# A transformer block on one core: from the fourth unit on, the feed-forward reads the finished second norm in 256 columns instead of the unscaled x in 258

## The chip, the cores and the metric

The kernel runs on one core of a Trainium2 chip, as one program with one launch. The metric is the time of one execution on the device in microseconds. A core has a matrix engine (TensorE; PE in the profile, PEld for its weight loads), a vector engine (VectorE; DVE), a scalar engine (ScalarE; ACT), GpSimd (POOL) and the queue of the sync engine that issues the loads (SP).

## The reference, cut to what matters

One block over 256 tokens with 1024 features, in float32: a modulated mixing part (attention and a gated unit), and then the feed-forward that the change touches:

```
x = x + gate1 * (merged @ w_out)
h = rmsnorm(x, g_ffn) * (1 + scale2) + shift2
x = x + gate2 * (square(relu(h @ w_ff1)) @ w_ff2)      # w_ff1: 1024 x 4096
return rmsnorm(x, g_final)
```

`rmsnorm` divides each token by the root of the mean square of its features, so `h` can only be finished when all features of `x` are known; `scale2` and `shift2` are one number per feature.

## The kernel before, in words

All data lie transposed: features on the 128 partitions in 8 tiles (`KT`), the 256 tokens along the row. To keep float32 accuracy each operand of a product is split in a rounded high part and a low remainder, and each product is three matmuls, high by high, high by low, low by high (`mm3`, line 72). The weights come as 1 MB pieces of 128 x 2048 in a fixed order of "slots": a load from the SP queue into one of five `raw` buffers, a cast to the high part on ScalarE (`high`, line 240, four buffers), and a subtraction on VectorE for the low part (`low`, line 249, three buffers). `prepare(slot + 2)` issues the low part of the slot after next and the high part of the one two further.

The feed-forward has 16 units of 256 hidden features. A unit has a first product (`ff1`, line 619: 8 feature tiles x 2 halves x 3 = 48 matmuls), an activation (`relu2` and `relu2_low`, lines 630 and 644) and a second product (`ff2`, line 651, 48 matmuls) that adds into four PSUM banks which stay for all units. On TensorE the order is: first products of units 1, 2, 3, then in turn second product of unit 1, first of unit 4, second of unit 2, first of unit 5, and so on. In the loop of line 683 iteration n holds the second product of unit n+1 and the first of unit n+4.

The first products don't wait for the norm. They read `zh`, `zl`: `x` times the norm's gain and (1 + scale2), not divided by the root, with 2 columns more per row (258): column 256 holds `shift2`, so that the matmul also gives the product of the shift, and column 257 is zero. Each half of the unit has its own bank. `relu2` mends the rest behind the product: it copies the shift's column out of the bank (`bw`), multiplies the bank by the tokens' factor `rb2` on VectorE, adds `bw` in a Relu on ScalarE, squares on ScalarE into `r2`, and casts that to `fh`; `relu2_low` makes the remainder `fl` on VectorE. `rb2` is there from the middle of the second unit's first product on (`spread2`).

`wide` (line 404) is the same product over rows of 256 columns, with both halves in one bank; the earlier stages use it, the output projection with `mh`, `ml`, which lie in the places `b1` and `b2`.

In this part the instructions are not pinned to the order of the program: a planner orders each engine's queue ahead of time, by the order of the program among what it takes to be ready. An engine then works off its queue in that order.

Of the kernel before, what the change touches and what calls it, by code (L numbers as in the profile page):

```python
# [9 lines left out]
F32 = mybir.dt.float32  # L10
F32R = mybir.dt.float32r
BF16 = mybir.dt.bfloat16
AF = mybir.ActivationFunctionType
ALU = mybir.AluOpType
AX = mybir.AxisListType

P = 128
S = 256
D = 1024
KT = D // P  # L20
# [27 lines left out]
def block_kernel(ctx, tc, x, xT, cols, wsguT, bsgu, w_a1, w_1, w_a, w_m, w_f, out):  # L48
    nc = tc.nc
    PE, DVE, ACT = (InOrder(tc, e) for e in (nc.tensor, nc.vector, nc.scalar))  # L50
    const = ctx.enter_context(tc.tile_pool(name="const", bufs=1))
    act = ctx.enter_context(tc.tile_pool(name="act", bufs=1))
    wk = ctx.enter_context(tc.tile_pool(name="wk", bufs=2))
# [6 lines left out]
    def bank():  # L60
        return ps.tile([P, 512], F32, name="bank", tag="bank")
# [8 lines left out]
    def mm3(out, wh, wl, ah, al, first, last, **kw):  # L70
        PE.matmul(out=out, lhsT=wh, rhs=ah, start=first, stop=False, **kw)
        PE.matmul(out=out, lhsT=wh, rhs=al, start=False, stop=False, **kw)
        PE.matmul(out=out, lhsT=wl, rhs=ah, start=False, stop=last, **kw)
# [11 lines left out]
    x_sb = act.tile([P, KT, S], F32, name="x_sb")  # L85
# [11 lines left out]
    def spin(n):  # L97
# [13 lines left out]
        out=maskf, in_=maskf, pattern=[[0, 2], [-1, P]], compare_op=ALU.is_ge,  # L111
# [60 lines left out]
    acol = const.tile([P, 2, KT], F32, name="acol")  # L172
    bcol = const.tile([P, 2, KT], F32, name="bcol")
    gcol = const.tile([P, 2, KT], F32, name="gcol")
    pre = const.tile([P, 2, KT], F32, name="pre")
    for n, (sc, g) in enumerate(((SCALE1, G_MIX), (SCALE2, G_FFN))):
        DVE.scalar_tensor_tensor(
            out=pre[:, n], in0=cols_sb[:, sc:sc + KT], scalar=1.0, in1=cols_sb[:, g:g + KT],
            op0=ALU.add, op1=ALU.mult)
# [60 lines left out]
    def high(n):  # L240
        if n < NM + 2 * NU:
            raw = fetch("w", n)
            hi = his.tile([P, 2048], F32R, name="whi", tag="whi")
            m = 2048 // pieces(n)
            for i in range(pieces(n)):
                ACT.copy(out=hi[:, m * i:m * i + m], in_=raw[:, m * i:m * i + m])
            his_of[n] = raw, hi

    def low(n):
        if n < NM + 2 * NU:  # L250
            raw, hi = his_of.pop(n)
            lo = los.tile([P, 2048], F32R, name="wlo", tag="wlo")
            m = 2048 // pieces(n)
            for i in range(pieces(n)):
                w = slice(m * i, m * i + m)
                DVE.tensor_tensor(out=lo[:, w], in0=raw[:, w], in1=hi[:, w].bitcast(F32), op=ALU.subtract)
            parts[n] = hi, lo

    def prepare(n):
        low(n)  # L260
        high(n + 2)

    def ada_dots(m, half):
        i = (0, 4, 1, 5, 2, 6, 3, 7, 8, 9, 10, 11, 12, 13, 14, 15)[m]
        if half == 0:
            raw_of["d", m] = fetch("a", m)
        raw = raw_of["d", m]
        column(dot(raw, half), (SCALE2, GATE1, SHIFT2, GATE2)[i // 4], 2 * (i % 4) + half)
# [11 lines left out]
    for kt in range(KT):  # L280
        f, l = kt == 0, kt == KT - 1
# [8 lines left out]
        hf = wk.tile([P, S], F32, name="hf", tag="hf", bufs=2)  # L290
        wp = [slice(2048 // np_ * i, 2048 // np_ * (i + 1)) for i in range(np_)]
        xk = xps[0][:, 0:S] if f else xn[:, kt]
        a, b = acol[:, 0, kt:kt + 1], bcol[:, 0, kt:kt + 1]
# [110 lines left out]
    def wide(n, ah, al, nk, base=0):  # L404

        wh, wl = parts[n]
        o = bank()
        for ko in range(nk):
            for i in range(2):
                w = slice(base + 256 * ko + P * i, base + 256 * ko + P * i + P)  # L410
                mm3(o[:, S * i:S * i + S], wh[:, w], wl[:, w], ah[:, ko], al[:, ko],
                    ko == 0 and i == 0, ko == nk - 1, skip_group_check=i == 1)
        return o
# [87 lines left out]
    sc, ex, tp, po, zo = {}, {}, {}, {}, {}  # L501
    A0, S0, TD, OD = 1, 5, 2, 3
    for n in range(10):
# [9 lines left out]
        if n == 2:  # L513
            nc.sync.dma_start(out=wsg, in_=wsguT)
            for i in range(2):
                nc.sync.dma_start(
                    out=bsg[64 * i:64 * i + 64],
                    in_=bass.AP(tensor=bsgu.tensor, offset=128 * i, ap=[[0, 64], [256, NP], [1, P]]))
            nc.gpsimd.affine_select(
                out=wsg, in_=wsg, pattern=[[0, 8], [1, P]], compare_op=ALU.is_ge,  # L520
# [9 lines left out]
        o = wide(n, hh, hl, KT)  # L530
# [18 lines left out]
        if n < 2:  # L549
            dst, func, scale = u_sb[:, 2 * n:2 * n + 2], AF.Gelu_apprx_tanh, 1.0  # L550
        else:
            dst, func, scale = (ga_sb, gb_sb)[m // 4][:, 2 * (m % 4):2 * (m % 4) + 2, 0:S], AF.Tanh, 0.5
# [5 lines left out]
    for j in range(4):  # L558
        n = 10 + j
        prepare(n + 2)  # L560
        t = []
        if n in AT:
            ada_dots(AT.index(n), 0)
        for k, (ah, al, g) in enumerate(((oh, ol, ga_sb), (yh, yl, gb_sb))):
            o = wide(n, ah, al, 4, 1024 * k)
            y = wk.tile([P, 2, S], F32, name="yg", tag=f"t512{'ab'[k]}")
            DVE.scalar_tensor_tensor(out=y, in0=g[:, 2 * j:2 * j + 2, 0:S], scalar=1.0,
                                     in1=o.rearrange("p (i t) -> p i t", i=2), op0=ALU.add, op1=ALU.mult)
# [15 lines left out]
    for j in range(4):  # L584
        n = 14 + j
# [4 lines left out]
        o = wide(n, mh, ml, KT)  # L590
# [5 lines left out]
        fts = (2 * j, 2 * j + 1)  # L596
        for ft in fts:
            i = ft % 2
            DVE.scalar_tensor_tensor(
                out=x_sb[:, ft], in0=o[:, S * i:S * i + S], scalar=gcol[:, 0, ft:ft + 1], in1=x_sb[:, ft],  # L600
                op0=ALU.mult, op1=ALU.add)
# [3 lines left out]
        for ft in fts:  # L605
            DVE.scalar_tensor_tensor(
                out=zl[:, ft, 0:S], in0=x_sb[:, ft], scalar=acol[:, 1, ft:ft + 1],
                in1=zh[:, ft, 0:S].bitcast(F32), op0=ALU.mult, op1=ALU.subtract)
# [7 lines left out]
    rb2 = const.tile([P, S], F32, name="rb2", tag="m1")  # L616
    slot = NM

    def ff1(n, half=None):
        wh, wl = parts[n]  # L620
        o = [bank(), bank()]
        for ko in range(KT):
            for i in range(2):
                w = slice(256 * ko + P * i, 256 * ko + P * i + P)
                mm3(o[i][:, 0:ZW], wh[:, w], wl[:, w], zh[:, ko], zl[:, ko], ko == 0, ko == KT - 1)
            if ko == 3 and half:
                half()
        return o

    def relu2(o):  # L630
        r = wk.tile([P, 2, S], F32, name="r", tag="t512a")
        bw = small.tile([P, 2], F32, name="bw", tag="bw")
        r2 = wk.tile([P, 2, S], F32, name="r2", tag="t512b")
        fh = wk.tile([P, 6 * P], F32R, name="fh", tag="pr", bufs=3)[:, 0:512].rearrange("p (i t) -> p i t", i=2)
        for i in range(2):
            DVE.tensor_copy(out=bw[:, i:i + 1], in_=o[i][:, S:S + 1])
            DVE.tensor_tensor(out=r[:, i], in0=o[i][:, 0:S], in1=rb2, op=ALU.mult)
        for i in range(2):
            ACT.activation(out=r[:, i], in_=r[:, i], func=AF.Relu, bias=bw[:, i:i + 1])
        ACT.activation(out=r2, in_=r, func=AF.Square)  # L640
        ACT.copy(out=fh, in_=r2)
        return r2, fh

    def relu2_low(r2, fh):
        fl = wk.tile([P, 6 * P], F32R, name="fl", tag="pt")[:, 0:512].rearrange("p (i t) -> p i t", i=2)
        DVE.tensor_tensor(out=fl, in0=r2, in1=fh.bitcast(F32), op=ALU.subtract)
        return fh, fl

    acc = []

    def ff2(n, fts, wp, a, first, last):
        wh, wl = wp
        fh, fl = a
        if not acc:
            acc.extend(bank() for _ in range(4))
        for ft in fts:
            o = acc[ft // 2][:, S * (ft % 2):S * (ft % 2) + S]
            for i in range(2):
                w = slice(1024 * i + P * ft, 1024 * i + P * ft + P)
                mm3(o, wh[:, w], wl[:, w], fh[:, i], fl[:, i], first and i == 0 and ft % 2 == 0,  # L660
                    last and i == 1, skip_group_check=ft % 2 == 1)

    f = {}
    a = {}
# [13 lines left out]
    a[0] = relu2(f.pop(0))  # L678
    slot += 1
    prepare(slot + 2)  # L680
    a[1] = relu2(f.pop(1))
    a[0] = relu2_low(*a[0])
    f[2] = ff1(slot)
    slot += 1
    for n in range(NU - 2):
        prepare(slot + 2)
        a[n + 1] = relu2_low(*a[n + 1])
        if n in (1, 3, 5, 7):
            ada_dots(12 + n // 2, 0)
        ff2(n, range(KT), parts[slot], a.pop(n), n == 0, False)  # L690
        a[n + 2] = relu2(f.pop(n + 2))
        slot += 1
        if n + 3 < NU:
            prepare(slot + 2)
            if n in (1, 3, 5, 7):
                ada_dots(12 + n // 2, 1)
            f[n + 3] = ff1(slot)
            slot += 1
    a[NU - 1] = relu2_low(*a[NU - 1])

# [6 lines left out]
    for j in range(4):  # L707
        fts = (2 * j, 2 * j + 1)
# [3 lines left out]
        for i, ft in enumerate(fts):  # L712
            DVE.scalar_tensor_tensor(out=x_sb[:, ft], in0=acc[j][:, S * i:S * i + S], scalar=gcol[:, 1, ft:ft + 1],
                                     in1=x_sb[:, ft], op0=ALU.mult, op1=ALU.add)
# [84 lines left out]
```

## Time and profile before

| | |
|---|---|
| time, median of 3 runs | 362.6 us (362.24 to 362.86) |
| time of the profiled execution | 363.53 us |
| span of the profiled execution, first to last instruction | 360.8 us |
| TensorE busy | 350.1 us, 97% of the span, 2898 matmuls |
| VectorE busy | 259.3 us, 72% |
| ScalarE busy | 216.7 us, 60% |
| GpSimd busy | 9.2 us, 3% |
| TensorE's mean granted clock | 0.996 of full speed (2.4 GHz) |

Busy times are sums of the union of an engine's instructions over the span; the shares are averages over stages with different limits. The duration of one matmul in the rows (0.28 us) holds its way through the array, and the next starts before it ends: what a stream of matmuls costs is read from the distance of their starts.

### The profile page before, as it was taken

To read this page: it belongs to the slowest core of one execution; us is meant where nothing else is said; L and a number is where in the kernel's file an instruction comes from. 1 tells how busy PE (TensorE), PEld (TensorE's weight loads), DVE (VectorE), ACT (ScalarE), POOL (GpSimd) and SP (SyncE) were. 2 spreads that over 40 slices of the span, in tenths; PEclk is the share of its full clock that TensorE was granted. 3 is DMA by queue.
4 is the path that set the end of the run, shared out by engine and by line. 5 is a ranking of instruction groups with operands and counts; after the bars stand their busy time and mean duration, and the time that the engine had idled before them with its cause. 6 is when DMAs were issued, how large, how long until landed. Compare 5 with 4: busy or idle time off the path is not lost.

```text
span 360.8 us, 6952 instructions
## 1 busy us (share of the span) xinstructions
PE 350.1 (97%) x2898; PEld 338.8 (94%) x2898; DVE 259.3 (72%) x403; ACT 216.7 (60%) x308; POOL 9.2 (3%) x16
## 2 busy tenths in 40 slices
PE   6999999999999999999999999999999999999993
PEld 5688989999999999999999999999999999999993
DVE  4898986689799988999858665576665654645443
ACT  5867679899954563555576554466544664446242
POOL 3000000003000000000000000000000000000001
PEclk9999999999999999999999999999999999999998
DMA  7999999699898896478554665746758464500003
GB/s 241 417 411 411 410 400 420 221 369 369 336 385 320 308 382 233 182 261 328 225 184 167 234 250 217 288 179 243 252 207 295 173 234 155 196 2 0 2 0 116
DMA packets 16270, 90.39 MB, mean 251 GB/s; under 512 B 1904, under 2 KB 2416, under 8 KB 7152
## 3 DMA queue, kind: packets, MB, share of 16 engines
q1 hardware_dynamic: 16240, 89.97, 66.4%
q8 instruction: 22, 0.36, 0.4%
q14 instruction: 8, 0.07, 0.1%
HBM read 88.91 MB, written 1.05 MB: 249 GB/s over the span
## 4 chain that ended last, share of the span: by engine, by line
PE 87%; DMA 6%; DVE 2%; issue 1%; SPq 1%; ACT 1%; POOLq 0%; POOL 0%; DVEq 0%
PE bank L44 87%; DMA raw<-in_w 3%; DMA raw<-in_w_a 3%; SPq L67 1%; DVE wlo L44 1%; DVE yg L44 0%; ACT whi L44 0%; DVE x_sb L44 0%; SPq L82 0%; DVE ys L44 0%; POOLq L795 0%; POOL sq L722 0%; DVE sq L44 0%; DVEq L795 0%; ACT sqt L44 0%
## 5 line engine op out<-in xcount | busy, mean ns | idle before, releaser
L44 ACT CAST whi<-raw 128x2048 fp32r<-128x2048 f32 (+2 forms) x74 | 113.2, 1540 | 81.7 <-PE bank L44 71.9
L44 DVE TENSOR_TENSOR wlo<-raw,whi 128x2048 fp32r<-128x2048 f32 (+2 forms) x80 | 134.9, 1700 | 12.3 <-ACT whi L44 12.1
L44 PE MATMUL bank<-zh,whi 128*128 128x258 f32 x256 | 72.6, 284 | 0.0
L44 PE MATMUL bank<-zl,whi 128*128 128x258 f32 x256 | 72.5, 283 | 0.0
L44 PE MATMUL bank<-zh,wlo 128*128 128x258 f32 x256 | 72.1, 282 | 0.0
L44 PE MATMUL bank<-fh,whi 128*128 128x256 f32 x256 | 70.7, 276 | 0.0
L44 PE MATMUL bank<-fh,wlo 128*128 128x256 f32 x256 | 70.7, 276 | 0.0
L44 PE MATMUL bank<-fl,whi 128*128 128x256 f32 x256 | 70.7, 276 | 0.0
L44 DVE SCALAR_TENSOR_TENSOR junk<-raw,csb 128x1024 bf16<-128x1024 f32 x48 | 57.4, 1218 | 0.6 <-DMA raw<-in_w_a 0.6
L44 PE MATMUL bank<-hh,whi 128*128 128x256 f32 x224 | 54.6, 283 | 0.8 <-ACT hh L44 0.7
L44 PE MATMUL bank<-hl,whi 128*128 128x256 f32 x224 | 53.7, 279 | 0.3 <-DVE hl L44 0.3
L44 PE MATMUL bank<-hh,wlo 128*128 128x256 f32 x224 | 53.5, 278 | 0.0
L44 PEld LDWEIGHTS bank<-zh,wlo 128*128 128x128 f32 x256 | 48.5, 190 | 0.0
L44 PEld LDWEIGHTS bank<-zh,whi 128*128 128x128 f32 x256 | 48.4, 189 | 0.0
L44 PEld LDWEIGHTS bank<-zl,whi 128*128 128x128 f32 x256 | 48.4, 189 | 0.0
L44 PEld LDWEIGHTS bank<-fh,whi 128*128 128x128 f32 x256 | 48.1, 188 | 0.0
L44 PEld LDWEIGHTS bank<-fl,whi 128*128 128x128 f32 x256 | 48.1, 188 | 0.0
L44 PEld LDWEIGHTS bank<-fh,wlo 128*128 128x128 f32 x256 | 48.1, 188 | 0.0
L44 PEld LDWEIGHTS bank<-hh,whi 128*128 128x128 f32 x224 | 38.5, 188 | 3.6 <-ACT hh L44 2.3
L44 PEld LDWEIGHTS bank<-hl,whi 128*128 128x128 f32 x224 | 38.3, 189 | 0.6 <-DVE hl L44 0.5
L44 PEld LDWEIGHTS bank<-hh,wlo 128*128 128x128 f32 x224 | 38.1, 188 | 0.1
L44 DVE TENSOR_TENSOR fl<-r,fh 128x512 fp32r<-128x512 f32 x16 | 11.1, 692 | 27.4 <-PE bank L44 26.1
(143 smaller groups left out, 475.2 us busy)
## 6 DMA issues: line engine op xcount, KB each, us to landing
raw<-in_w_f SPq DMA_DIRECT2D x32, 1024.0 KB, 4.8
raw<-in_w_a SPq DMA_DIRECT2D x22, 1024.0 KB, 6.8
raw<-in_w_m SPq DMA_DIRECT2D x16, 1024.0 KB, 5.5
raw<-in_w SPq DMA_DIRECT2D x12, 512.0 KB, 9.5
raw<-in_w_a SPq DMA_DIRECT2D x4, 512.0 KB, 7.4
raw<-in_w SPq DMA_DIRECT2D x8, 256.0 KB, 7.7
xt<-in_x SPq DMA_DIRECT2D x2, 512.0 KB, 3.9
raw<-in_w_m SPq DMA_DIRECT2D x4, 256.0 KB, 6.3
```

What stands on the lines that cost most here:

```text
L44: return lambda *a, **k: pin(op(*a, **k))
L67: nc.sync.dma_start(out=t[:, n * i:n * i + n], in_=src[:, n * i:n * i + n])
```

## The change

Two tiles `nh`, `nl` of 8 x 256 columns take the places b1 and b2. A new function `full` makes them, per feature tile, from `x`, `rb2`, the scale and the shift: the finished `h`, split in a high and a low part. It is called for tiles 0 and 1 ahead of the second unit's activation, for 2 to 4 behind the first product of unit 3, and for 5 to 7 behind the second product of unit 1. From unit 4 on the first product is `wide` over `nh`, `nl` (256 columns, one bank), and the activation is a new function `square`: Relu out of the bank on ScalarE, `r2` as a product on VectorE, and `fh` as a Square on ScalarE. Units 1 to 3 stay as they were.

```diff
--- before.py
+++ after.py
@@ -646,6 +646,29 @@
         DVE.tensor_tensor(out=fl, in0=r2, in1=fh.bitcast(F32), op=ALU.subtract)
         return fh, fl
 
+
+    nh = act.tile([P, KT, S], F32R, name="nh", tag="b1")
+    nl = act.tile([P, KT, S], F32R, name="nl", tag="b2")
+
+    def full(fts):
+        for ft in fts:
+            sc, sh = acol[:, 1, ft:ft + 1], bcol[:, 1, ft:ft + 1]
+            xb = wk.tile([P, S], F32, name="xb", tag="hf", bufs=2)
+            DVE.tensor_tensor(out=xb, in0=x_sb[:, ft], in1=rb2, op=ALU.mult)
+            ACT.activation(out=nh[:, ft], in_=xb, func=AF.Identity, scale=sc, bias=sh)
+            DVE.tensor_scalar(out=xb, in0=xb, scalar1=sc, scalar2=sh, op0=ALU.mult, op1=ALU.add)
+            DVE.tensor_tensor(out=nl[:, ft], in0=xb, in1=nh[:, ft].bitcast(F32), op=ALU.subtract)
+
+    def square(o):
+
+        r2 = wk.tile([P, 2, S], F32, name="r2", tag="t512b")
+        fh = wk.tile([P, 6 * P], F32R, name="fh", tag="pr", bufs=3)[:, 0:512].rearrange("p (i t) -> p i t", i=2)
+        r = wk.tile([P, 2, S], F32, name="r", tag="t512a")
+        ACT.activation(out=r, in_=o.rearrange("p (i t) -> p i t", i=2), func=AF.Relu)
+        DVE.tensor_tensor(out=r2, in0=r, in1=r, op=ALU.mult)
+        ACT.activation(out=fh, in_=r, func=AF.Square)
+        return r2, fh
+
     acc = []
 
     def ff2(n, fts, wp, a, first, last):
@@ -678,9 +701,11 @@
     a[0] = relu2(f.pop(0))
     slot += 1
     prepare(slot + 2)
+    full(range(0, 2))
     a[1] = relu2(f.pop(1))
     a[0] = relu2_low(*a[0])
     f[2] = ff1(slot)
+    full(range(2, 5))
     slot += 1
     for n in range(NU - 2):
         prepare(slot + 2)
@@ -688,13 +713,15 @@
         if n in (1, 3, 5, 7):
             ada_dots(12 + n // 2, 0)
         ff2(n, range(KT), parts[slot], a.pop(n), n == 0, False)
-        a[n + 2] = relu2(f.pop(n + 2))
+        if n == 0:
+            full(range(5, KT))
+        a[n + 2] = (square if n else relu2)(f.pop(n + 2))
         slot += 1
         if n + 3 < NU:
             prepare(slot + 2)
             if n in (1, 3, 5, 7):
                 ada_dots(12 + n // 2, 1)
-            f[n + 3] = ff1(slot)
+            f[n + 3] = wide(slot, nh, nl, KT)
             slot += 1
     a[NU - 1] = relu2_low(*a[NU - 1])
 
```

## Rows read from the trace of the kernel before

**Rows 1.** Page, parts 1 and 2: engines, and TensorE's granted clock by slice

```profile
PE 350.1 (97%) x2898; PEld 338.8 (94%) x2898; DVE 259.3 (72%) x403; ACT 216.7 (60%) x308; POOL 9.2 (3%) x16
...
PEclk9999999999999999999999999999999999999998
```

**Rows 2.** Waits of TensorE, whole run: total, times, longest

```profile
PE bank L44 <- DVE identb L44: 3.2, 1, 3.2
...
PE bank L44 <- ACT mh L44: 0.2, 1, 0.2
```

**Rows 3.** Windows: stretch, its length, busy time (instructions) of each engine, clock, DMA

```profile
182.25:199.70 17.45, 17.45 (x150) 17.45 (x150) 11.72 (x17) 11.84 (x15) 0.00 (x0) 1.00 0.46 165
206.00:240.00 34.00, 34.00 (x294) 34.00 (x293) 22.07 (x31) 18.09 (x19) 0.00 (x0) 1.00 0.68 253
```

**Rows 4.** Timeline of TensorE: start, duration; first product unit 4, second unit 2

```profile
194.98 0.29 PE L44 MATMUL bank<-zh,whi 128*128 128x258 f32 x1
...
200.62 0.28 PE L44 MATMUL bank<-zh,wlo 128*128 128x258 f32 x1
200.74 0.28 PE L44 MATMUL bank<-fh,whi 128*128 128x256 f32 x1
...
206.19 0.29 PE L44 MATMUL bank<-zh,whi 128*128 128x258 f32 x1
```

**Rows 5.** Timeline of TensorE: 256-column products of `wide` in earlier stages

```profile
65.41 0.28 PE L44 MATMUL bank<-hl,whi 128*128 128x256 f32 x1
...
70.83 0.28 PE L44 MATMUL bank<-hh,wlo 128*128 128x256 f32 x1
...
153.57 0.50 PE L44 MATMUL bank<-mh,whi 128*128 128x256 f32 x2 [0.16 <-ACT mh L44]
...
159.80 0.28 PE L44 MATMUL bank<-mh,whi 128*128 128x256 f32 x1
...
171.25 0.28 PE L44 MATMUL bank<-mh,wlo 128*128 128x256 f32 x1
```

**Rows 6.** Groups of VectorE, 182.25 to 199.7: count, busy, mean, idle before

```profile
L44 DVE TENSOR_TENSOR wlo<-raw,whi 128x2048 fp32r<-128x2048 f32 x3 | 6.9, 2284 | 0.0
L44 DVE TENSOR_TENSOR fl<-r,fh 128x512 fp32r<-128x512 f32 x3 | 2.1, 688 | 2.6 <-ACT fh L44 1.3 <-PE bank L44 1.3
L44 DVE TENSOR_TENSOR r<-bank,rb 128x256 f32<-128x256 f32 x4 | 1.7, 414 | 0.0
```

**Rows 7.** Groups of ScalarE, 182.25 to 199.7 us

```profile
L44 ACT CAST whi<-raw 128x2048 fp32r<-128x2048 f32 x3 | 5.7, 1913 | 1.8 <-PE bank L44 1.8
```

**Rows 8.** Groups of all engines, 190 to 361 us

```profile
L44 DVE TENSOR_TENSOR sq<-sq,sqt 128x512 f32<-128x512 f32 x2 | 1.4, 691 | 1.4 <-ACT sqt L44 1.4
...
L44 ACT ACTIVATE ys<-bank,rs 128x512 f32<-128x512 f32 x2 | 1.3, 683 | 0.8 <-POOL rs L127 0.8
...
L44 DVE TENSOR_SCALAR yg<-x_sb,cols_sb 128x256 f32<-128x256 f32 x2 | 0.6, 347 | 0.0
```

**Rows 9.** Groups of VectorE, 150 to 182 us

```profile
L44 DVE SCALAR_TENSOR_TENSOR zl<-x_sb,acol,zh 128x256 fp32r<-128x256 f32 x8 | 3.5, 479 | 0.0
...
L44 DVE TENSOR_TENSOR sq<-sq,sqp 128x256 f32<-128x256 f32 x6 | 2.5, 421 | 0.0
```

**Rows 10.** Groups of ScalarE, 150 to 182 us

```profile
L44 ACT ACTIVATE zh<-x_sb,acol 128x256 fp32r<-128x256 f32 x8 | 3.6, 500 | 0.0
```

**Rows 11.** Timeline of VectorE, units 1 to 4

```profile
181.49 0.76 DVE L44 TENSOR_TENSOR r<-bank,rb 128x256 f32<-128x256 f32 x2 [1.80 <-ACT rb L44]
...
200.66 0.41 DVE L44 TENSOR_TENSOR r<-bank,rb 128x256 f32<-128x256 f32 x1
201.00 2.29 DVE L44 TENSOR_TENSOR wlo<-raw,whi 128x2048 fp32r<-128x2048 f32 x1
...
206.35 0.69 DVE L44 TENSOR_TENSOR fl<-r,fh 128x512 fp32r<-128x512 f32 x1 [1.27 <-PE bank L44]
```

**Rows 12.** Waits of all engines, 195 to 340 us

```profile
ACT whi L44 <- PE bank L44: 55.6, 25, 3.8
```

## The prediction

> **What bounds the kernel now.** I read the page's engine table and slices first: TensorE is busy 97% of the span at its full granted clock, and no other engine is near that [rows 1]. Then the waits of TensorE over the whole run: four entries, the largest of 3.2 us early on, none of them in the feed-forward [rows 2]. Then two stretches by engine: from 206 to 240 us, TensorE is busy all 34.0 us while VectorE has 22.1 and ScalarE 18.1 [rows 3]. So from the first unit of the feed-forward to the second products of the last, the time is the number of matmuls times the spacing of their starts; work of the other engines costs something only where a matmul comes to wait for it.
>
> So the view that prices the change is the timeline of TensorE: where each product starts [rows 4]. The first product of unit 4 (48 matmuls of 258 columns) starts at 194.98 and the second product behind it (48 of 256) at 200.74: 5.76 us, or 120.0 ns a matmul. The second product lasts until 206.19: 5.45 us, or 113.5 ns. Two columns in 258 are 0.8%; the spacing differs by 5.7%. This pair of figures repeats in every unit up to the end.
>
> **The change part by part.**
>
> *First products of units 4 to 16 (thirteen).* Each keeps its 48 matmuls, and they lose two columns, the odd row length of 258 and the second bank. I price them by the same `wide` reading `mh` and `ml`, which lie in the very places (tags b1, b2) that `nh` and `nl` will have, with the same weight layout: 102 matmuls from 159.80 to 171.25, 101 steps, 113.4 ns [rows 5]. That is the spacing of the second products too. Saving: 13 x 48 = 624 matmuls x (120.0 - 113.5) = 624 x 6.5 ns = 4.06 us; by starts of products, 13 x (5.76 - 5.45) = 4.03 us. I take 4.0. The bounds: a 256-column `wide` reading `hh` ran at 117.8 ns in some units (65.41 to 70.83, 46 steps [rows 5]), which would leave 624 x 2.2 = 1.4 us; and if each column costs the same (113.5 / 256 = 0.44 ns), two columns are worth 0.9 ns and the whole 0.55 us. I stay with 113.5, the row that is nearest in function, place and neighbours.
>
> *The Trainium skill on this.* "TensorE: Matmul & The Clock Gate", section "Back-to-back issue gap", gives the isolated gap of a warm matmul as the columns over 2.4 plus 2.5 ns, so two columns would be worth 0.83 ns and the change, as an estimate from that page, 0.52 us. The trace has 6.5 ns between its two widths, eight times as much, and the sum goes by the trace.
>
> *Making `nh`, `nl` (`full`, eight tiles).* Added on VectorE per tile: a multiply (nearest row 421 ns), a two-scalar operation in place (between the one-scalar 347 ns [rows 8] and the 479 ns of a three-operand one [rows 9]; I take 420), a subtract (421). Queued back to back each costs less, since starts follow at 0.34 us where the duration is 0.41 [rows 11]: 0.34 + 0.36 + 0.34 = 1.04 us a tile, 8.3 for eight. ScalarE gets eight Identity operations at 500 ns [rows 10], 4.0 us. This must be ready before unit 4 reads it. `rb2` is there for use when unit 1's two scalings run, 181.49 to 182.25 [rows 11]; the first product of unit 4 starts at 194.98, and its last eighth, which reads the last tile, 7/8 of 5.45 us later, at 199.75. In that window of 17.45 us VectorE is now busy 11.72 us and ScalarE 11.84 [rows 3]. With the new work: 20.0 and 15.8. So VectorE has 2.5 us too much in this window; but not all of its 11.72 us is due there. Due are the scaling of unit 2 (half of 1.7 us), two of the three weight remainders `wlo` (2.2 us each at their spacing) and two of the three `fl` [rows 6]: 0.8 + 4.4 + 1.2 = 6.4 us. The third `wlo`, the third `fl`, the dot of the modulation and the scaling of unit 3 are needed only when later products start, from 206.19 on. By that count the last `nl` could be done at 182.25 + 6.4 + 8.3 = 197.0, 2.8 us early. The planner fills gaps in order of the program, and in the program the tiles stand ahead of all four of these.
>
> What eats the 2.8 us: each tile crosses from VectorE to ScalarE and back, and while ScalarE is in a 1.9 us cast of weights [rows 7] the third operation of a tile waits, with all of VectorE's queue behind it (`wlo`, `fl`). The planner can put another tile's multiply there, since `xb` has two buffers, or start a 2.3 us `wlo` in the gap and so delay the tile. Bounds of the wait on TensorE: none at the one end. At the other, no overlap at all: 0.42 + 0.50 + 0.42 + 0.42 and three handovers of some 0.04 are 1.9 us a tile, 15.2 for eight, behind the whole 11.72: done at 209.2, 9.4 us late. The rows due are nearest to the early end; two or three handovers behind a cast cost most of the 2.8 us of slack, so I take 0.3 us of waiting, in the last two tiles.
>
> *`square` in place of `relu2` (units 4 to 16).* Per unit VectorE loses two copies and two scalings and gains a product of 691 ns; ScalarE has one Relu out of the bank (nearest row: 683 ns [rows 8]) and one Square instead of four operations. None of it is on the path: the chain cast 1.9, Relu 0.7, product 0.7, remainder 0.7 ends 4.0 us after the first product, at 204.7 for unit 4, where `fl` now starts only at 206.35 because its buffer is released by TensorE [rows 11], and its reader starts a whole unit later. Worth 0; if that cover were gone it could not cost more than the chain.
>
> *Moved or delayed.* `wlo` for slot 24 may slip by some 2 us behind the tiles; its reader starts at 206.19, and the load that it releases feeds a cast that now waits for TensorE each time (55.6 us in 25 waits [rows 12], no wait for a DMA among them). Cost 0. The change issues no DMA. `yg` and `ys` now reuse the places of `nh` and `nl`, whose last reader ends before the last second products. Cost 0. The thirteen products use one bank each instead of two: nothing waits for a bank now, so worth 0.
>
> *Sum.* -4.03 + 0.3 = -3.7 us. The profiled execution: span 360.8 - 3.7 = 357.1, time 363.5 - 3.7 = 359.8. It was 0.9 us above the median of the runs shown, so against that median 362.6 - 3.7 = 358.9 us.
>
> **The rivals.**
>
> *A. A real wait at unit 4.* The tiles come late and TensorE stands. For it: 20.0 us of VectorE work in a window of 17.45. Against: 5 us of that can be put off, and the planner can give TensorE the next second product meanwhile. If everything in the window runs ahead of the last tile, it is 2.5 us late: 362.6 - 4.0 + 2.5 = 361.1. Only a wait of 4.0 us or more eats the gain; the far end gives 362.6 - 4.0 + 9.4 = 368.0.
>
> *B. The slow spacing (the other side).* Of the 256-column products that read `hh`, some ran at 113.5 and some at 117.8 ns, each from its first to its last matmul, after TensorE had been broken off by other work. If the wait at unit 4 sets off the 117.8 ns and nothing resets it, all matmuls to the end pay 4.3 ns: 13 first and 15 second products, 28 x 48 = 1344 x 4.3 = 5.8 us, and 362.6 - 4.0 + 0.3 + 5.8 = 364.7. It decides from 940 such matmuls on (4.03 us / 4.3 ns). Against: the one wait inside a like stream, for `mh` at 153.57, was followed by 113.4 ns [rows 5], and every second product has come at 113.5, whatever went before.
>
> *C. The slow spacing in the first products alone.* 1.4 us are saved: 361.2. For it the same rows; against it `mh`.
>
> *D. It doesn't do what it says.* The 6.5 ns belong to something other than width, row length and bank, and only two columns' worth goes: 362.6 - 0.55 + 0.3 = 362.3. Against: the weights, the function and the neighbours of a first product are those of products at 113.5.
>
> **How the numbers follow.** The forecast, a wait under 1 us and 113.5 ns: 68%, 358.5 to 359.6. A with a wait of 1 to 3.3 us: 12%, up to 361.9. A with more: 5%, of which 2 within 0.2% and 3 slower. B: 6%. C: 5%. D: 4%. About 0.2%, or 0.7 us, is what a measurement of this kernel can tell from no change. Faster: 68 + 12 + 5 = 85%. Same: 2 + 4 = 6%. Slower: 3 + 6 = 9%. The range, 358.0 to 361.4, holds the forecast, most of A's shorter waits and C.
>
> **What would show it.** Thirteen first products of 256 columns that last 5.45 us each from start to start, and a feed-forward with no stop but one under 1 us near 195 to 200 us, in which TensorE waits for `nl` or `nh`: right. Spacing of 120 in them, or 117.8 there and behind: D, C or B. A wait of several us at unit 4 with VectorE's queue full: A. TensorE waiting for `fl` or `wlo` in later units would show that I costed the rest wrongly at nothing. The prediction is wrong if the time is above 361.4 or below 358.0.

## The result, and the profile after

The changed kernel takes 359.63 us (median of 6 runs, 359.42 to 360.94) where the kernel before takes 362.46 (6 runs): ratio 0.9921, 95% interval 0.9907 to 0.9935, or 2.8 us less. In a later comparison it was 359.13 against 362.67 (0.9902, 0.9885 to 0.992), 3.5 us less. The forecast was 358.9 in a range of 358.0 to 361.4. Single executions of one and the same kernel can lie some us apart, and the section on the hardware shows what one such execution looks like inside.

The profiled execution took 360.94 us with a span of 359.1 (before: 363.53 and 360.8). Its page opens with the busy times; the waits of TensorE over the whole run now have an entry in the feed-forward (who waited <- for whom: total, times, longest):

```profile
PE 347.7 (97%) x2898; PEld 336.3 (94%) x2898; DVE 266.0 (74%) x388; ACT 206.9 (58%) x290; POOL 7.3 (2%) x16
```

```profile
...
PE bank L44 <- DVE nl L44: 0.6, 1, 0.6
```

The timeline of TensorE answers to [rows 4]: the first product of unit 1, which opens the feed-forward, at 172.93, unit 4's from 196.55 us on, its last matmuls among those of the second product of unit 2, then unit 5's and the second product behind it, and the start of the last second products.

```profile
172.93 0.29 PE L44 MATMUL bank<-zh,whi 128*128 128x258 f32 x1
...
196.55 0.28 PE L44 MATMUL bank<-nh,whi 128*128 128x256 f32 x1
...
200.63 0.28 PE L44 MATMUL bank<-nh,whi 128*128 128x256 f32 x1
201.55 0.39 PE L44 MATMUL bank<-nl,whi 128*128 128x256 f32 x1 [0.65 <-DVE nl L44]
...
204.01 0.33 PE L44 MATMUL bank<-nl,whi 128*128 128x256 f32 x1
...
208.49 0.28 PE L44 MATMUL bank<-nh,whi 128*128 128x256 f32 x1
...
213.93 0.28 PE L44 MATMUL bank<-fh,whi 128*128 128x256 f32 x1
...
333.61 0.28 PE L44 MATMUL bank<-fh,whi 128*128 128x256 f32 x1
```

Three things are to be seen. A first product of 256 columns lasts 213.93 - 208.49 = 5.44 us, 113.3 ns a matmul, where one of 258 took 5.76 [rows 4]. From the first product of unit 5 to the last second products it is 125.12 us; before, that stretch ran from 206.19 [rows 4] to 335.30, 129.11 us. So the twelve first products in it, with their neighbours, give 4.0 us. But from unit 4's first product to unit 5's it is 11.94 us, where before it was 206.19 - 194.98 = 11.21: 0.73 lost in place of 0.32 gained, so the wait and what goes with it cost 1.05. TensorE stands from 200.63 to 201.55 where 0.11 would do (0.8 us), and matmuls behind it (14 from 202.36 to 204.01) come at 117.8 ns. The last five matmuls of this first product, those for tile 7, stand inside the second one, at 204.01: that is where the planner put them.

The feed-forward as a whole went from 171.36 to 335.30 before, and from 172.93 to 333.61 after: 163.94 to 160.68 us, 3.3 less. The span fell by only 1.7, since in this execution the stages ahead, which the change doesn't touch, ended 1.6 us later. The two ends of the stretch before:

```profile
171.36 0.29 PE L44 MATMUL bank<-zh,whi 128*128 128x258 f32 x1
...
335.30 0.28 PE L44 MATMUL bank<-fh,whi 128*128 128x256 f32 x1
```

VectorE's timeline shows why the last tiles, 6 and 7 (counted from 0), are late. Each tile is a multiply into `xb`, an Identity on ScalarE that gives `nh`, a second operation on `xb` in place, and the subtraction that gives `nl`; the last of these frees the buffer of `xb`:

```profile
197.54 0.42 DVE L44 TENSOR_TENSOR xb<-x_sb,rb 128x256 f32<-128x256 f32 x1
197.88 0.42 DVE L44 TENSOR_TENSOR nl<-xb,nh 128x256 fp32r<-128x256 f32 x1
198.22 2.29 DVE L44 TENSOR_TENSOR wlo<-raw,whi 128x2048 fp32r<-128x2048 f32 x1
200.42 0.41 DVE L44 TENSOR_SCALAR xb<-xb,acol,bcol 128x256 f32<-128x256 f32 x1
200.74 0.42 DVE L44 TENSOR_TENSOR xb<-x_sb,rb 128x256 f32<-128x256 f32 x1
201.07 0.42 DVE L44 TENSOR_TENSOR nl<-xb,nh 128x256 fp32r<-128x256 f32 x1
...
203.48 0.42 DVE L44 TENSOR_TENSOR nl<-xb,nh 128x256 fp32r<-128x256 f32 x1
```

Tile 6's multiply is the one at 197.54. Its Identity waited behind a cast on ScalarE (below), so its next operation on VectorE could not follow. Tile 7's multiply could not fill the gap at once either: with two buffers it needs the one that tile 5's `nl`, started at 197.88, frees at 198.30. The planner filled the gap from 198.22 on with a weight remainder of 2.29 us for unit 5's first product, which starts only at 208.49. Tile 7's multiply follows at 200.74. The `nl` at 201.07 is tile 6's, for which TensorE waits; tile 7's is ready only at 203.90.

```profile
197.09 1.90 ACT L44 CAST whi<-raw 128x2048 fp32r<-128x2048 f32 x1
198.89 0.60 ACT L44 ACTIVATE nh<-xb,bcol,acol 128x256 fp32r<-128x256 f32 x1
```

### The profile page after: what moved, and what is told of

Its sections match the earlier page's. It is cut to its first block, busy times and chain, and to the rows that moved or that the text cites. A ratio compares the mean times of both kernels' runs of the same rounds, so it can differ in the third digit from the quotient of the medians.

```text
span 359.1 us, 6908 instructions
## 1 busy us (share of the span) xinstructions
PE 347.7 (97%) x2898; PEld 336.3 (94%) x2898; DVE 266.0 (74%) x388; ACT 206.9 (58%) x290; POOL 7.3 (2%) x16
## 3 DMA queue, kind: packets, MB, share of 16 engines
HBM read 88.91 MB, written 1.05 MB: 251 GB/s over the span
## 4 chain that ended last, share of the span: by engine, by line
PE 74%; ACT 8%; DVE 6%; DMA 6%; issue 2%; SPq 1%; POOL 0%; POOLq 0%; DVEq 0%; ACTq 0%
PE bank L44 74%; DVE wlo L44 3%; DMA raw<-in_w 3%; DMA raw<-in_w_a 3%; ACT whi L44 2%; ACT pr L44 2%; ACT L44 1%; DVE xb L44 1%; SPq L67 1%; ACT vs_sb L44 1%; DVE nl L44 1%; ACT r L44 1%; DVE r L44 0%; ACT v_sb L44 0%; DVE x_sb L44 0%
## 5 line engine op out<-in xcount | busy, mean ns | idle before, releaser
L44 ACT CAST whi<-raw 128x2048 fp32r<-128x2048 f32 (+2 forms) x74 | 113.1, 1539 | 94.6 <-PE bank L44 84.5
L44 PE MATMUL bank<-nl,whi 128*128 128x256 f32 x208 | 57.6, 277 | 0.6 <-DVE nl L44 0.6
L44 PE MATMUL bank<-nh,whi 128*128 128x256 f32 x208 | 57.4, 276 | 0.0
L44 PE MATMUL bank<-nh,wlo 128*128 128x256 f32 x208 | 57.4, 276 | 0.0
L44 PEld LDWEIGHTS bank<-nl,whi 128*128 128x128 f32 x208 | 39.0, 188 | 0.8 <-DVE nl L44 0.8
L44 PEld LDWEIGHTS bank<-nh,whi 128*128 128x128 f32 x208 | 39.0, 188 | 0.0
L44 PEld LDWEIGHTS bank<-nh,wlo 128*128 128x128 f32 x208 | 39.0, 188 | 0.0
```

The source lines that it names most:

```text
L44: return lambda *a, **k: pin(op(*a, **k))
```

## The experiments

The theory: the gain is 13 first products at 0.32 us, and what is missing from 4.0 us is the wait at unit 4 and nothing else. The rivals: the making of the tiles costs by itself; or the missing part lies in the activation or the banks.

**Without the making.** All products as in the changed kernel, but nothing is made: `full` and its calls are left out.

```diff
...
-            f[n + 3] = wide(slot, nh, nl, KT)
+            f[n + 3] = wide(slot, mh, ml, KT)
```

> Leaves out the making of the finished norm: the first products of units 4 to 16 read the tiles of the output projection (mh, ml) in 256 columns, so the numbers are another function's; all else is as in the changed kernel. Theory: the changed kernel's gain is the spacing of 13 first products (13 x 0.32 = 4.0 us) less about 1 us at unit 4, where TensorE waited 0.8 us for the last tile of nl and went on at a wider spacing for a while. Without the making there is nothing to wait for: 362.5 - 4.0 = 358.5 us, 1.1 below the changed kernel, no wait of TensorE after 170 us. Rival: the shortfall against 4.0 us lies elsewhere (square, banks, one longer product); then this kernel stays at 359.6.

Measured: 358.59 us (5 runs; before beside it 362.67; ratio 0.9885, 0.9861 to 0.9909), no wait of TensorE in the feed-forward, all products from unit 4 on at 5.43 to 5.45 us (113.1 to 113.5 ns a matmul). 4.1 us are saved, as good as the whole of 13 x 0.32. So what the changed kernel lacks comes with the making: by its work, or by a wait for it.

**Made and not used.** The changed kernel with the products and activations of before.

```diff
-        a[n + 2] = (square if n else relu2)(f.pop(n + 2))
+        a[n + 2] = relu2(f.pop(n + 2))
...
-            f[n + 3] = wide(slot, nh, nl, KT)
+            f[n + 3] = ff1(slot)
```

> The kernel before with the eight tiles of the finished norm made at the same places in the program and read by nobody. Theory: 0.0 to 0.2 us over the kernel before (362.5), since TensorE waits for nothing of it. Rival: the making costs about 1 us by itself: 363.5.

Measured: 362.69 us (12 runs), before 362.67; ratio 0.9992, 0.997 to 1.0013. The rival's 1 us would be 0.3% and lies outside the interval, which ends at 0.13%. The eight tiles cost nothing that shows as work; they cost what waits for them.

**Used from unit 5 on.**

```diff
-        a[n + 2] = (square if n else relu2)(f.pop(n + 2))
+        a[n + 2] = (square if n > 1 else relu2)(f.pop(n + 2))
...
-            f[n + 3] = wide(slot, nh, nl, KT)
+            f[n + 3] = wide(slot, nh, nl, KT) if n else ff1(slot)
```

> The changed kernel with the finished norm read from unit 5 on; unit 4 still reads the unscaled x in 258 columns. Theory: the tiles are then ready 11 us ahead of their first reader, so the wait of about 1 us goes, and one product's 0.32 us is not gained: 12 x 0.32 = 3.8 us, 362.5 - 3.8 = 358.7 us, 0.9 below the changed kernel. Rival: the making costs by itself, wait or not (the weight remainders on VectorE come late and TensorE waits for them later): 359.6 or more.

Measured: 358.70 us (358.21 to 359.40, 4 runs), ratio 0.9884 (0.9858 to 0.991); no wait. The next two ran it and the changed kernel side by side.

> The kernel that reads the finished norm from unit 5 on, once more, beside the changed kernel on one chip. Theory: 358.7 us, 0.9 below the changed kernel. Rival: the difference of the first comparison was between chips; then both are alike within 0.3 us.

> The changed kernel itself, for the comparison on one chip. Theory: 359.6 us, one wait of TensorE for nl of some 0.8 us at unit 4. Rival: 358.7, if the difference was between chips.

Measured: 358.79 (358.51 to 359.01) from unit 5, 359.13 (358.94 to 359.29) for the changed kernel, 362.67 for before. The order is the expected one and the two sets of runs hardly overlap, but the distance is 0.3 us, not 0.9, and 0.3 is what the rival allowed. So the medians alone don't settle it, and the price of the wait is read from the traces. In the two profiled executions the feed-forward up to the last second products took 331.58 - 171.63 = 159.95 us and 331.77 - 171.08 = 160.69: 0.74 apart, which is the 1.05 of the wait less unit 4's 0.32. The changed kernel's stages ahead had ended 0.55 us sooner there.

**The tiles together, earlier in the program.**

```diff
-    full(range(2, 5))
+    full(range(2, KT))
...
-        if n == 0:
-            full(range(5, KT))
```

> The changed kernel with all of tiles 2 to 7 made at one place of the program, directly behind unit 3's first product, so that the planner takes them ahead of a weight remainder of 2.3 us that stood in front of the last two tiles. Theory: the wait at unit 4 shrinks or goes: 358.4 to 358.8 us. Rival: VectorE has too much to do in that window whatever the order, and a wait of about 0.8 us stays: 359.6.

Measured: 359.62 us (ratio 0.9901, 0.9877 to 0.9926); the same wait of 0.65 us. A wait of the rival's size stayed, so the place in the program doesn't help. But it is not shown that VectorE has too much to do: the planner put the same weight remainder (2.28 us, at 197.13) ahead of the last two tiles. The profiled execution took 365.67 us and is read in the section on the hardware.

**The multiplies on GpSimd.**

```diff
-            DVE.tensor_tensor(out=xb, in0=x_sb[:, ft], in1=rb2, op=ALU.mult)
+            (DVE if ft < 2 else nc.gpsimd).tensor_tensor(out=xb, in0=x_sb[:, ft], in1=rb2, op=ALU.mult)
```

> The changed kernel with the multiply of x by the tokens' factor for tiles 2 to 7 on GpSimd, which is idle there, instead of VectorE: 6 x 0.34 = 2.0 us less on VectorE in the window before unit 4. Theory: VectorE's load in that window makes the last tile late by 0.8 us; with 2.0 us less the wait goes, and all thirteen products gain: 362.5 - 4.0 = 358.4 us. Rival: the handovers between the engines set it, and GpSimd's slower multiply adds to them: a wait of 0.8 us or more stays, 359.6.

Measured: 363.37 us (12 runs), ratio to before 1.0009 (0.9988 to 1.0031): the whole gain is lost. The rival came, and worse: in the profiled execution the wait of TensorE for `nl` grew to 2.3 us. That execution took 368.41 us, so its rows are read for the mechanism alone. VectorE's timeline:

```profile
187.64 0.68 DVE L44 TENSOR_TENSOR fl<-r,fh 128x512 fp32r<-128x512 f32 x1
188.25 0.83 DVE L44 TENSOR_SCALAR xb<-xb,acol,bcol 128x256 f32<-128x256 f32 x1
...
189.66 0.83 DVE L44 TENSOR_SCALAR xb<-xb,acol,bcol 128x256 f32<-128x256 f32 x1
...
191.15 0.40 DVE L44 TENSOR_SCALAR xb<-xb,acol,bcol 128x256 f32<-128x256 f32 x1
191.47 2.83 DVE L44 TENSOR_TENSOR wlo<-raw,whi 128x2048 fp32r<-128x2048 f32 x1
...
196.97 1.76 DVE L44 SCALAR_TENSOR_TENSOR junk<-raw,csb 128x1024 bf16<-128x1024 f32 x1
```

and GpSimd's beside it:

```profile
187.80 1.12 POOL L657 TENSOR_TENSOR xb<-x_sb,rb 128x256 f32<-128x256 f32 x1 [0.36 <-DVE nl L44]
189.61 0.74 POOL L657 TENSOR_TENSOR xb<-x_sb,rb 128x256 f32<-128x256 f32 x1 [0.69 <-DVE nl L44]
191.31 0.85 POOL L657 TENSOR_TENSOR xb<-x_sb,rb 128x256 f32<-128x256 f32 x1 [0.96 <-DVE nl L44]
...
196.79 0.85 POOL L657 TENSOR_TENSOR xb<-x_sb,rb 128x256 f32<-128x256 f32 x1 [0.96 <-DVE nl L44]
```

Beside five of the six GpSimd multiplies an instruction of VectorE is longer by 0.42 to 0.55 us: 0.82 or 0.83 for 0.40 (three times), 2.83 for 2.28, 1.76 for 1.22; beside the sixth an `nl` takes 0.57 for 0.42. Together that is 2.5 us, so the 2.0 us were not taken off VectorE, and each multiply still waits for a buffer that `nl` frees. Twice, where an `fl` on VectorE had started first (187.64 and 194.56, 0.68 each, as elsewhere), the multiply itself took 1.12 us. (The Trainium skill, "SBUF — State Buffer", section "SBUF: two separate sides", says that the two engines share a pair of ports, and that whichever starts first holds it for the whole instruction; these rows agree, in that the one that is longer than elsewhere is each time the one that started later.)

**Four buffers.**

```diff
-            xb = wk.tile([P, S], F32, name="xb", tag="hf", bufs=2)
+            xb = wk.tile([P, S], F32, name="xb", tag="hf", bufs=4)
```

(and the same count at the two other tiles of that tag).

> The changed kernel with four buffers instead of two for the tile xb in which each piece of the norm is made, so that VectorE's multiplies run ahead and the planner puts the last pieces in front of the 2.3 us weight remainder instead of behind it. Theory: VectorE had the time for all eight tiles; the wait at unit 4 came from two buffers and the remainder taken in between. The wait goes, thirteen products gain 0.32 us each: 362.6 - 4.1 = 358.5 us, no wait of TensorE behind 170 us, and no execution at 117.8 ns to the end. Rival: the load of VectorE in the window sets it, whatever the buffers: a wait of 0.6 us or more stays, 359.1 to 359.6.

Measured: 358.42 us (358.01 to 359.98, 6 runs), before 362.69 beside it; ratio 0.9882, 0.986 to 0.9904. The theory holds. VectorE's timeline has the last tiles ahead of the remainder:

```profile
196.26 0.75 DVE L44 TENSOR_TENSOR nl<-xb,nh 128x256 fp32r<-128x256 f32 x2
...
197.33 2.28 DVE L44 TENSOR_TENSOR wlo<-raw,whi 128x2048 fp32r<-128x2048 f32 x1
```

and TensorE goes from unit 4 to the end without a stop, 25 products in 136.00 us, 5.44 each:

```profile
194.97 0.28 PE L44 MATMUL bank<-nh,whi 128*128 128x256 f32 x1
...
330.97 0.28 PE L44 MATMUL bank<-fh,whi 128*128 128x256 f32 x1
```

The last `nl` is ready at 197.0. In the changed kernel above it was ready at 203.9, with a feed-forward that had begun 1.6 us later; that leaves 5.3 us sooner, from the same work. This version beats the kernel before; it was not timed beside the changed kernel, whose medians were 0.7 to 1.2 us higher.

**What makes the 6.5 ns.** The kernel before with another form of first product in each unit.

```diff
+    FORMS = ((zh, zl, 256), (ml, ml, 256), (wx, wx, 258), (wx, wx, 260), (wx, wx, 264), (wx, wx, 272),
+             (wx, wx, 288), (wx, wx, 256), (ml, ml, 240), (ml, ml, 192), (ml, ml, 254), (zh, zl, 258),
+             (ml, ml, 256))
...
-            f[n + 3] = ff1(slot)
+            f[n + 3] = first(slot, *FORMS[n])
```

> Measures the disputed 6.5 ns by itself. The kernel before, whose first products of units 4 to 16 read other tiles in other forms, two banks each as before, with a shortened activation (another function's numbers; units in order: 256 columns of the 258-long rows of zh; 256 of rows of 256; 258, 260, 264, 272, 288 of rows of 288; 256 of rows of 288; 240, 192, 254 of rows of 256; 258 of 258; 256 of 256). Theory: the width over 256 alone makes the wider spacing: 113.4 ns at 256 whatever the row length and with two banks, 120 at 258 in rows of 288, and at least 120 from there on; below 256 the spacing stays near 113 if weight loads set it, or falls by 0.42 ns a column if the columns do. Rival one: the row length of 258 does it: 120 at 256 of 258-long rows, 114.3 at 258 of 288. Rival two: the two banks: 120 at 256 of 256 as well.

The timeline of TensorE, where some of these products start and the second product behind each:

```profile
196.48 0.28 PE L44 MATMUL bank<-zh,whi 128*128 128x256 f32 x1
202.19 0.28 PE L44 MATMUL bank<-fh,whi 128*128 128x256 f32 x1
207.62 0.39 PE L44 MATMUL bank<-ml,whi 128*128 128x256 f32 x2
213.06 0.28 PE L44 MATMUL bank<-fh,whi 128*128 128x256 f32 x1
218.50 0.40 PE L44 MATMUL bank<-wx,whi 128*128 128x258 f32 x2
224.26 0.28 PE L44 MATMUL bank<-fh,whi 128*128 128x256 f32 x1
...
303.00 0.30 PE L44 MATMUL bank<-fh,whi 128*128 128x256 f32 x1
308.68 0.40 PE L44 MATMUL bank<-ml,whi 128*128 128x254 f32 x2
314.36 0.28 PE L44 MATMUL bank<-fh,whi 128*128 128x256 f32 x1
```

By start to start over 48 matmuls: 256 columns of 258-long rows 119.0 ns; 256 of 256 with two banks 113.3; 258 of 288-long rows 120.0; 260, 264, 272, 288 of them 119.6, 121.2, 125.0, 132.7; 256 of 288-long rows 116.0; 240, 192 and 254 of 256-long rows 111.9, 111.3 and 118.3. So the theory of the width alone falls, and so do both rivals alone: the two banks cost nothing, the row length of 258 costs 5.7 ns even at 256 columns, and 258 columns cost 6.7 even in rows of 288 (4.0 against 256 columns of the same rows). By these single products either is enough, and the change removes both. 240 and 192 columns save little, at 111.9 and 111.3 ns. Each form ran in one product of one execution, and 256 columns have a second, wider rhythm of 117.8 ns (below), which four of the second products took here. The 118.3 of 254 columns stands between two of these (from 303.00 and 314.36 on), so it doesn't show that 254 are slower than 256. The 119.0 of the row length lies near that rhythm too, so that reading is the weaker of the two, though its steps are as uneven as those of 258 columns (0.11 to 0.13 us, where the wider rhythm has 0.11 and 0.12 alone).

## Why the prediction was right, and where it missed

- *The bound and the gain*: right. Spacing of 120.0 and then 113.3 ns, 0.32 us a product against the 0.31 taken from the `mh` rows; without the wait the kernels with 13 such products saved 4.1 to 4.3 us against 4.03. The estimate from the Trainium skill ("TensorE: Matmul & The Clock Gate", section "Back-to-back issue gap"), 0.52 us, is far below all of these; the page has that formula for an isolated matmul, and says itself that in a stream of weight loads and matmuls both set the spacing. The cause that I named beside it was only half worked out: by the single products width and row length each suffice, and the bank does not count.
- *`square`, the banks, the moved work at 0*: right. The kernel without the making lost nothing to them, and no unit after the fourth shows a wait.
- *The wait*: the term that was mis-sized. I took 0.3 us "in the last two tiles"; it was 0.8 us of standing and 1.05 with what followed, for tile 6 (the last but one). With 1.05 in its place the sum is 3.0 us saved, between the 2.8 and the 3.5 measured. The step that failed is "the planner fills gaps in order of the program, and in the program the tiles stand ahead of all four of these": the planner let a remainder of 2.3 us in ahead of the last two tiles, though it stands behind them in the program, because the two buffers kept the next multiply from being ready. I had named that as a possibility and priced it too low. With four buffers the last `nl` came at 197.0, where the count had put it, so the count of the work was right and the order was wrong. That it agrees to the tenth is in part luck: one of unit 3's two scalings, which the count had put off, ran ahead of the last tile as well (at 194.94), and the tiles themselves took a little less than counted.
- *Rival A*, what speaks against it ("the planner can give TensorE the next second product meanwhile"): that is what it did for tile 7, whose `nl` came only at 203.9. Its five matmuls stand behind 14 of the second product, at 204.01 and not at 202.36. Had they stood in their place, TensorE would have stood 1.5 us more, and the wait would have been three times as long.
- *Rival B* was held at 6%. It is no invention: in one of five executions of the kernel with the tiles together, behind the same wait of 0.65 us, and in the profiled one with GpSimd, the matmuls ran at 117.8 ns to the end. The changed kernel's ten runs (358.94 to 360.94 us) show none at that price, but no run shows what spared them; that they were spared was in part luck.

## What to carry to other kernels

When TensorE has no gap, price a change of a matmul's form by the distance of starts of a like form in the trace, not by its columns: here two columns, in rows two elements longer, cost 6%. Work that is hidden must be in time for its first reader as the queues are really ordered; with two buffers between engines, a planner that fills gaps can put a long instruction in the wrong gap, as here. A wait in a stream of matmuls can cost more than its length, since the stream may go on at a wider spacing, so the first use of new data is better put one step later or its buffers widened than left to a close finish.

## What the runs showed of the hardware

A stream of 256-column matmuls showed two rhythms here, that is two distances from start to start, 113.4 and 117.8 ns, and kept the one that it had until something else came between. The same instructions take either from one execution to the next: the projections that read `oh` and `yh`, untouched here, started 2.72 us apart (113.4 ns) in the kernel before:

```profile
127.41 0.28 PE L44 MATMUL bank<-oh,whi 128*128 128x256 f32 x1
...
130.13 0.28 PE L44 MATMUL bank<-yh,whi 128*128 128x256 f32 x1
...
149.17 0.28 PE L44 MATMUL bank<-mh,whi 128*128 128x256 f32 x1
```

In the changed kernel's profiled execution they started 2.83 us apart (117.8), and in its profiled execution of the later comparison 2.72 again (127.12 to 129.84). The first of these two:

```profile
128.11 0.28 PE L44 MATMUL bank<-oh,whi 128*128 128x256 f32 x1
...
130.94 0.28 PE L44 MATMUL bank<-yh,whi 128*128 128x256 f32 x1
...
150.72 0.28 PE L44 MATMUL bank<-mh,whi 128*128 128x256 f32 x1
```

From `oh` to the start of `mh` it is 22.61 us here and 149.17 - 127.41 = 21.76 before. That is 0.85 us of scatter with no wait in it. In the profiled execution of the kernel with the tiles together the wide rhythm, once set behind the wait, stayed to the end; the stretch from 208 to 330 us by engine, clock 1.00 in both, first that kernel and then the changed one:

```profile
208.00:330.00 122.00, 122.00 (x1038) 122.00 (x1037) 72.45 (x63) 54.16 (x44) 0.00 (x0) 1.00 0.57 206
```

```profile
208.00:330.00 122.00, 122.00 (x1079) 122.00 (x1078) 75.33 (x67) 56.33 (x45) 0.00 (x0) 1.00 0.56 207
```

122 us hold 1038 matmuls or 1079, all busy by the profile. What sets the rhythm I tried on the kernel without the making, with extra matmuls of one column between the products (one execution of each kernel):

```diff
+    def tiny():
+        PE.matmul(out=tb[:, 0:1], lhsT=ones, rhs=ones[:, 0:1], start=True, stop=True)
...
+            tiny()
             ff2(n, range(KT), parts[slot], a.pop(n), n == 0, False)
...
+            tiny()
             f[n + 3] = wide(slot, mh, ml, KT)
```

> The kernel without the making (first products of units 4 to 16 read mh, ml), with one extra matmul of one column (ones by ones, into a spare bank) ahead of each product from the first product of unit 4 on: 26 interruptions. It tests whether the spacing has two values that an interruption sets. Theory: after an interruption a whole product runs either at 113.4 or at 117.8 ns, and both occur, some 3 to 6 in 10 at 117.8. Rival: the wider spacing belongs to the waits and the shapes of the places where it was seen; then all 26 run at 113.4.

Measured: a whole product has one rhythm, as the theory has it, but by no chance: all thirteen first products at 117.8 and all thirteen second ones at 113.6, in turn. The timeline, with the extra matmul (two records) ahead of each:

```profile
195.08 0.36 PE L44 MATMUL bank<-mh,whi 128*128 128x256 f32 x1
...
200.82 0.28 PE L44 MATMUL bank<-ones 128*128 128x1 f32 x2
200.96 0.36 PE L44 MATMUL bank<-fh,whi 128*128 128x256 f32 x1
...
206.50 0.28 PE L44 MATMUL bank<-ones 128*128 128x1 f32 x2
```

From the first matmul of a product to the next extra one it is 5.74 us in the first product and 5.54 in the second. With one matmul of 258 columns behind each extra one (`PE.matmul(out=tb[:, 0:ZW], lhsT=zh[:, 0, 0:P], rhs=zh[:, 0], ...)`):

> The same with one matmul of 258 columns (zh by zh, into the spare bank) behind each extra matmul of one column. In the kernel before every 256-column product behind a 258-column one came at 113.4. Theory: 258 columns bring the stream back to 113.4, so all products behind run at 113.4. Rival: they don't, and as many run at 117.8 as with the one-column matmul alone.

Measured: all 26 at 117.8. The theory that 258 columns bring the stream back falls. With two extra matmuls of one column in place of one:

> The kernel without the making, with two extra matmuls of one column ahead of each product instead of one. With one, the first products all ran at 117.8 ns and the second ones all at 113.6, in turn. If it is the break in the stream that flips the spacing, they alternate here too: 13 at 117.8, 13 at 113.6. If it is the number of instructions between (their count modulo some power of two), two extra matmuls bring both to the same value: all 26 alike.

Measured: all 26 at 113.4; the same two rows of the timeline are 5.54 to 5.56 us apart in every product:

```profile
195.23 0.36 PE L44 MATMUL bank<-mh,whi 128*128 128x256 f32 x1
...
200.78 0.50 PE L44 MATMUL bank<-ones 128*128 128x1 f32 x4
```

So it is not the break as such that flips the rhythm; what is put between decides, at least here. Whether that is the number of instructions, their form or the length of the break (0.14 us with one extra matmul, 0.35 and 0.36 with two) these runs don't separate, and what chooses the rhythm behind a wait stays open.

Last, the clock. In the GpSimd kernel's profiled execution TensorE stood from 199.95 to 202.59 us, and then ran from 203.4 to 206.4 at a granted clock of 0.50, the lower level of 1.2 GHz, and at 1.00 again behind it:

```profile
203.40:206.40 3.00, 3.00 (x16) 3.00 (x15) 2.72 (x2) 2.91 (x3) 0.00 (x0) 0.50 0.71 300
206.60:210.40 3.80, 3.80 (x35) 3.80 (x34) 1.34 (x3) 0.00 (x0) 0.00 (x0) 1.00 0.86 304
```

Behind the changed kernel's stop of 0.9 us the granted clock stayed at 1.00 (200 to 206 us). The other executions of the GpSimd kernel, with a mean clock of 0.986 to 0.994 where the kernel before had 0.993 to 0.997 beside them, point the same way.
